# Two-layer trunk on one core: gate and up products of the MLP with the tokens stationary, turned back by 32x32 transposes and a pass through DRAM

## The chip, the core and the metric

The kernel runs on 1 core of one Trainium2 chip. The metric is the device time of one execution in microseconds (us); before the change the median of three runs is 2818.43 us (2815.97 to 2819.57).

## The reference, cut to what matters

The model is a trunk of two layers over 256 tokens of width 2048, all in float32. The part that the change concerns is the gated MLP, once per layer:

```python
D_MODEL = 2048; SEQ = 256; D_FF = 5632; CONV_WIDTH = 3

def causal_dwconv(u, w):          # depthwise over positions, width 3
    y = up[:, 0:L] * w[0]         # up: u with two zero rows in front
    for k in range(1, CONV_WIDTH):
        y = y + up[:, k:k + L] * w[k]
    return y

def conv_gated_mlp(h, w_gate, w_up, conv_w, conv_b, w_down):
    g = causal_dwconv(h @ w_gate, conv_w) + conv_b
    return (jax.nn.silu(g) * (h @ w_up)) @ w_down

def reference(...):
    for l in range(DEPTH):
...
        h = h + memory_cross_attention(rms_norm(h, norm_xattn[l]), mem_n, xa_w_q[l], xa_w_kv[l], xa_w_o[l])
        h = h + conv_gated_mlp(rms_norm(h, norm_ffn[l]), ff_w_gate[l], ff_w_up[l],
                               ff_conv_w[l], ff_conv_b[l], ff_w_down[l])
    return rms_norm(h, norm_final)
```

`rms_norm` divides each token by the root of its mean square and multiplies by a gain per channel. The mixers (a short convolution with an S5 scan in layer 0, sliding-window attention in layer 1) and the cross attention into 256 memory tokens stay as they are.

## The kernel before, in words

**Data.** Activations lie with channels on the 128 partitions and the 256 tokens along the free axis: the residual `h` is 16 tiles of 128x256. Weights are float32 in DRAM and are used once, so they stream: HBM reads come to 523 MB in the whole run.

**Precision.** Every product is computed from split operands. `wload` (lines 78-94) loads one block of weights (1 MB: 16 k of 128x128, or four k of 128x512) into a `raw` buffer by one DMA on SyncE's queue, and splits it in pieces of 1024 columns: ScalarE casts to `hi` (line 90, type float32r), VectorE takes the rest to `lo` (line 91). There are three raw buffers and four buffers each of hi and of lo pieces, enough for two blocks. Activations are split in the same way into operand tiles `op` of 128x512: hi in the first 256 columns, lo in the last (`split`, `split_gain`, lines 63-76; 32 such tiles).

**A tile of a product.** `gemm` (119-156) goes over output tiles of 128 channels. The weights are stationary and the tokens move: per k one matmul of hi against hi and lo of the tokens (line 105, 512 columns), then per k one of lo against hi of the tokens (line 110, 256 columns). The left and right halves of the PSUM bank are summed afterwards (`add_halves`, 158-161: a copy by ScalarE, an add by VectorE). There are four PSUM banks for this (`pp`) and four for all else (`pm`). Two parameters of `gemm` cover the end of the stage ahead: `pre` tiles are started with all k but the last `late`, which come after.

**The order.** The program is written as straight Python. The framework fixes the order of each engine's instructions ahead of time by its own model of durations, under the data dependences and the buffers that come free; it isn't program order. Each engine, and each DMA queue (SyncE's and ScalarE's), then works strictly in its order.

**The MLP** (`mlp`, 910-958) takes the 16 operand tiles `xs` of the normed residual. The norm's factor per token isn't in them: it is computed from sums of squares (`stat_add`, `stat_col`, `stat_bc`: 168-218) as a column per token and, by a small matmul, as a tile `rbc` that holds it along the tokens on every partition. `pairs` computes gate and up tile by turns. `evac_gate` (916-926) sums the halves, multiplies by rbc (GpSimd, line 919), convolves over tokens (lines 921-923), applies silu and multiplies by rbc again (line 925), since the up tile is taken unscaled; `evac_up` (928-932) sums its halves, multiplies by the gate's result (line 931) and splits it into an operand tile for the down product. The 44 channel tiles go in four slabs of 11; after each slab one pair of the next, then the down product over that slab's 11 k, added to `h` (`resid_part`, 960-963). The last slab's down product goes through `resid_evac` (279-295), which adds to `h`, squares for the next norm (line 174, summed by GpSimd in line 172) and, in layer 0, splits the next stage's operands (`split_gain`, lines 67 and 68).

**A product of the other form** stands in the cross attention's values (`mem_kv`, 311-329): there the memory tokens are stationary, 128 at a time, and weights 512 wide move. Per 512 channels there are two PSUM banks (tokens 0-127 and 128-255); each block of four k has 16 matmuls with hi weights (lines 319, 320) and 8 with lo (line 324). The result has tokens on partitions; ScalarE scales it by a factor per token on the way out of PSUM (line 328) and writes it to DRAM. That is done ahead of the layers, at 135 to 440 us.

## Time and profile before

| what | before |
|---|---|
| median of three runs | 2818.43 us |
| the profiled execution | 2817.71 us |
| its span, first to last instruction | 2815.9 us |
| granted TensorE clock, mean | 0.997 |
| instructions | 42249 |
| DMA packets, bytes, mean rate | 89788, 536.63 MB, 191 GB/s |
| queue of SyncE (q1), share of the 16 engines' time | 52.7% |
| queue of ScalarE (q10), the same | 0.9% |

A profile is of one execution. Engines in its rows: PE is TensorE's matmuls, PEld its loads of the stationary operand (beside the matmuls), DVE VectorE, ACT ScalarE, POOL GpSimd, SP SyncE; a q behind an engine's name is its sequencer or queue. L105 is line 105 of the kernel. A group of instructions reads: line, engine, operation, output<-inputs, shapes, count | busy us, mean ns of one | idle time of the engine just before them, and what ended it. A row of waits reads: who waited <- for whom: us in total, times, longest. A row of a time line reads: start, length, engine, line, operation, and how many are merged. Matmuls overlap in the records, so their pace is read from start to start. A row of windows reads: stretch, its length, busy us of PE, PEld, DVE, ACT and POOL with counts, granted clock, mean busy share of the 16 DMA engines, GB/s. A row of DMA issues reads: what, queue, count, KB each, median us from issue to landing.

### The profile page before, as it was taken

What the parts mean: (1) busy time and instruction counts of PE and PEld (TensorE: products, weight loads), DVE (VectorE), ACT (ScalarE), POOL (GpSimd) and SP (SyncE); (2) the same over time, 40 slices, a digit from 0 to 9 for tenths busy, and PEclk for the clock granted to TensorE, in tenths of its full rate; (3) what the DMA queues carried; (4) which work ended last, traced back from release to release, by engine and by line L of the source; (5) the groups of instructions that cost most, each with busy time, mean ns of one, the idle gap of its engine ahead of it and who ended that gap; (6) DMA issues with size and microseconds to landing.
All of it is one profiled execution on the core that took longest, in us unless ns stands there. A gap on an engine that the chain in (4) does not pass through costs nothing.

```text
span 2815.9 us, 42249 instructions
## 1 busy us (share of the span) xinstructions
PE 2785.6 (99%) x16263; PEld 2438.2 (87%) x16263; DVE 1975.3 (70%) x3227; ACT 1570.8 (56%) x2544; POOL 360.5 (13%) x397
## 2 busy tenths in 40 slices
PE   9999999999999999999999999999999999999998
PEld 8787878888988888888888888889888888888887
DVE  8978788867666666666666778776666666666666
ACT  7676766655555545545445566555555455454454
POOL 2000000000012211202112310000122022021122
PEclk9999999999999999999999999999999999999999
DMA  8664665555455545455454544454455554554544
GB/s 305 204 213 172 213 226 202 201 181 210 180 177 186 193 171 212 169 206 190 169 210 176 198 171 163 150 211 179 174 185 190 174 205 168 209 192 168 206 171 143
DMA packets 89788, 536.63 MB, mean 191 GB/s; under 512 B 10641, under 2 KB 17137, under 8 KB 38641
## 3 DMA queue, kind: packets, MB, share of 16 engines
q1 hardware_dynamic: 86656, 524.66, 52.7%
q10 hardware_dynamic: 2928, 9.26, 0.9%
q8 instruction: 127, 2.08, 0.3%
q14 instruction: 77, 0.62, 0.1%
HBM read 523.35 MB, written 10.53 MB: 190 GB/s over the span
## 4 chain that ended last, share of the span: by engine, by line
PE 94%; DVE 3%; ACT 2%; DMA 1%; issue 1%; POOL 0%; SPq 0%; DVEq 0%; ACTq 0%; POOLq 0%
PE ps L105 55%; PE ps L110 29%; PE ps L319 2%; PE ps L324 2%; PE ps L320 2%; DVE lo L91 1%; PE m L882 1%; PE m L788 1%; ACT stmp L489 1%; ACT hi L90 1%; DMA kv<-kst 0%; PE m L774 0%; DVE S L494 0%; PE m L742 0%; PE m L852 0%
## 5 line engine op out<-in xcount | busy, mean ns | idle before, releaser
L105 PE MATMUL ps<-op,hi 128*128 128x512 f32 x6997 | 1689.3, 392 | 5.4 <-ACT hi L90 2.8
L105 PEld LDWEIGHTS ps<-op,hi 128*128 128x128 f32 x6997 | 1283.2, 188 | 260.5 <-ACT hi L90 5.2
L91 DVE TENSOR_TENSOR lo<-raw,hi 128x1024 fp32r<-128x1024 f32 (+2 forms) x1033 | 1200.6, 1185 | 378.4 <-ACT hi L90 154.8
L90 ACT CAST hi<-raw 128x1024 fp32r<-128x1024 f32 (+2 forms) x1033 | 1001.8, 983 | 813.0 <-PE ps L105 720.5
L110 PEld LDWEIGHTS ps<-op,lo 128*128 128x128 f32 x7008 | 903.6, 191 | 38.5 <-DVE lo L91 2.3
L110 PE MATMUL ps<-op,lo 128*128 128x256 f32 x7008 | 920.5, 283 | 1.3 <-DVE lo L91 1.3
L172 POOL TENSOR_TENSOR acc<-acc,t 128x256 f32<-128x256 f32 x98 | 90.8, 927 | 1185.7 <-ACT t L174 1181.7
L160 ACT COPY t<-ps 128x256 f32<-128x256 f32 x290 | 106.9, 370 | 166.5 <-PE ps L110 163.6
L919 POOL TENSOR_TENSOR t<-t,rbc 128x256 f32<-128x256 f32 x88 | 68.8, 781 | 748.7 <-DVE t L161 720.9
L922 DVE SCALAR_TENSOR_TENSOR t<-t,ff_conv 128x255 f32<-128x255 f32 x88 | 42.9, 487 | 141.9 <-ACT t L921 141.9
L925 POOL TENSOR_TENSOR t<-t,rbc 128x256 f32<-128x256 f32 x88 | 109.5, 1244 | 216.2 <-ACT t L924 216.2
L68 DVE SCALAR_TENSOR_TENSOR op<-h,gains,op 128x256 fp32r<-128x256 f32 x96 | 72.8, 765 | 85.1 <-ACT op L67 85.0
L489 ACT ACTIVATE stmp<-S,s_pw 128x256 f32<-128x256 f32 (+3 forms) x256 | 116.8, 522 | 27.6 <-DVE S L496 21.6
L75 DVE TENSOR_TENSOR op<-t,op 128x256 fp32r<-128x256 f32 x104 | 43.8, 425 | 118.6 <-ACT op L74 118.2
L161 DVE TENSOR_TENSOR t<-ps,t 128x256 f32<-128x256 f32 x250 | 103.8, 415 | 0.9 <-ACT t L160 0.9
L319 PE MATMUL ps<-hi,op 128*128 128x512 f32 x256 | 101.0, 394 | 0.3 <-ACT hi L90 0.2
L320 PE MATMUL ps<-hi,op 128*128 128x512 f32 x256 | 99.8, 390 | 0.0
L931 POOL TENSOR_TENSOR t<-t 128x256 f32<-128x256 f32 x88 | 67.2, 764 | 135.0 <-DVE t L161 134.7
L74 ACT CAST op<-t 128x256 fp32r<-128x256 f32 x104 | 41.9, 406 | 50.7 <-POOL t L931 43.3
L494 DVE TENSOR_TENSOR S<-S,stmp 128x512 f32<-128x512 f32 (+11 forms) x92 | 60.6, 663 | 13.0 <-ACT stmp L489 12.8
L324 PE MATMUL ps<-lo,op 128*128 128x512 f32 x256 | 63.6, 390 | 0.7 <-DVE lo L91 0.7
L921 ACT ACTIVATE t<-t,ff_b,ff_conv 128x256 f32<-128x256 f32 x88 | 52.3, 595 | 20.7 <-POOL t L919 20.7
(213 smaller groups left out, 1494.9 us busy)
## 6 DMA issues: line engine op xcount, KB each, us to landing
raw<-in_ff_gate SPq DMA_DIRECT2D x88, 1024.0 KB, 4.8
raw<-in_ff_up SPq DMA_DIRECT2D x88, 1024.0 KB, 4.8
raw<-in_ff_down SPq DMA_DIRECT2D x128, 704.0 KB, 4.0
raw<-in_xa_k SPq DMA_DIRECT2D x32, 1024.0 KB, 4.9
raw<-in_xa_v SPq DMA_DIRECT2D x32, 1024.0 KB, 5.3
raw<-in_xa_q SPq DMA_DIRECT2D x32, 1024.0 KB, 4.8
raw<-in_xa_o SPq DMA_DIRECT2D x32, 1024.0 KB, 4.8
raw<-in_ev_w_in SPq DMA_DIRECT2D x28, 1024.0 KB, 4.9
```

Of the source, the lines that this page charges most:

```text
L90: nc.scalar.copy(hi, s)
L91: nc.vector.tensor_tensor(lo, s, hi.bitcast(F32), op=ALU.subtract)
L105: nc.tensor.matmul(ps, lhsT=hi, rhs=o, start=k == 0, stop=False)
L110: self.nc.tensor.matmul(ps[:, :T], lhsT=w[k][1], rhs=ops[k][:, :T], start=False, stop=k == K - 1)
L160: self.nc.scalar.copy(t, ps[:, T:])
L161: self.nc.vector.tensor_tensor(out, ps[:, :T], t, op=ALU.add)
L172: nc.gpsimd.tensor_tensor(self.acc, self.acc, self.sq, op=ALU.add)
L319: nc.tensor.matmul(ps[b], lhsT=o[:, b * P:(b + 1) * P], rhs=w[j][0], start=k == 0, stop=False)
L320: nc.tensor.matmul(ps[b], lhsT=o[:, T + b * P:T + (b + 1) * P], rhs=w[j][0], start=False, stop=False)
L324: nc.tensor.matmul(ps[b], lhsT=self.memop[k][:, b * P:(b + 1) * P], rhs=w[j][1], start=False, stop=k == KT - 1)
L489: nc.scalar.activation(tmp[:, x, :, p - p0, :], at(0, both, p), AF.Copy, scale=pw[:, x, k, 8 * b + p:8 * b + p + 1])
L925: nc.gpsimd.tensor_tensor(y, y, self.rbc, op=ALU.mult)
```

## The change

Of the 44 channel tiles of gate and up, the first 40 (`NTOK`) are computed in 10 chunks of 512 channels with the tokens stationary; the last four stay as they were.

- The tokens stand in `xs` in even-odd order: first the 128 even tokens, then the 128 odd ones. `split_gain` and the last `resid_evac` of the cross attention write them so (reads with a step of two, writes contiguous). So `stat_col`, `stat_bc` and `add_halves` get a `turned` form that undoes or follows it.
- `tok_gemm` is the product: per 512 channels two banks (even and odd tokens), four blocks of weights, each of 16 matmuls with hi and 8 with lo, 512 columns moving in all of them. The weights of gate and up are packed for it as blocks of four k by 512 channels, 8 KB contiguous per partition as before.
- `tok_turn` brings the result back to channels on partitions: ScalarE copies each bank out, scaled by the norm's factor per token; VectorE transposes it in blocks of 32x32, writing even and odd tokens by turns; four DMAs on ScalarE's queue write it to DRAM, 32 partitions each, in pieces of 64 floats (256 B); one DMA on SyncE's queue reads it back as four channel tiles of 128x256, in pieces of 1 KB.
- Since the factor is applied on the way out of PSUM, GpSimd's two products with rbc fall away for these tiles. Convolution, silu, product and split stay.
- The slabs of the down product become 12, 12, 12 and 8 k; each comes one chunk (the last one four pairs) after the tiles that it uses. The last has `late=1, pre=2`.

The core of the diff:

```diff
-SLAB = 11
+NTOK = 40
...
+        self.dz = pool("dramz", 4, space=DRAM)
...
-    def split_gain(self, src, gcol):
+    def split_gain(self, src, gcol, turned=False):
         nc = self.nc
         o = self.op_tile()
-        nc.scalar.activation(o[:, :T], src, AF.Copy, scale=gcol)
-        nc.vector.scalar_tensor_tensor(o[:, T:], src, gcol, o[:, :T].bitcast(F32), op0=ALU.mult, op1=ALU.subtract)
+        hi, lo = o[:, :T], o[:, T:]
+        if turned:
+            src = src.rearrange("p (m b) -> p b m", b=2)
+            hi, lo = (x.rearrange("p (b m) -> p b m", b=2) for x in (hi, lo))
+        nc.scalar.activation(hi, src, AF.Copy, scale=gcol)
+        nc.vector.scalar_tensor_tensor(lo, src, gcol, hi.bitcast(F32), op0=ALU.mult, op1=ALU.subtract)
         return o
...
+    def tok_gemm(self, src, xs, after=None):
+        nc = self.nc
+        ps = [self.pp.tile([P, 512], F32, name="ps", tag="ps") for _ in range(2)]
+        for q in range(4):
+            w = self.wload(src(q), 4, 512)
+            for j in range(4):
+                k = 4 * q + j
+                for b in range(2):
+                    for i in range(2):
+                        nc.tensor.matmul(ps[b], lhsT=xs[k][:, i * T + b * P:i * T + (b + 1) * P], rhs=w[j][0], start=k == 0 and i == 0, stop=False)
+            for j in range(4):
+                k = 4 * q + j
+                for b in range(2):
+                    nc.tensor.matmul(ps[b], lhsT=xs[k][:, b * P:(b + 1) * P], rhs=w[j][1], start=False, stop=k == KT - 1)
+            if after is not None:
+                after(q)
+        return ps
+
+    def tok_turn(self, pool, ps, rcol, tag):
+        nc = self.nc
+        tt = pool.tile([P, 16, 32, 2], F32, name="tt", tag="tt")
+        for b in range(2):
+            z = pool.tile([P, 512], F32, name="zt", tag="zt")
+            nc.scalar.activation(z, ps[b], AF.Copy, scale=rcol[:, b:b + 1])
+            nc.vector.transpose(tt[:, :, :, b], z.rearrange("p (j i) -> p j i", i=32))
+        zd = self.dz.tile([512, T], F32, name="zd", tag="zd")
+        for q in range(4):
+            nc.scalar.dma_start(zd.rearrange("(j i) (q e) -> q i j e", i=32, q=4)[q], tt[32 * q:32 * q + 32].rearrange("p j i b -> p j (i b)"))
+        zf = pool.tile([P, 4, T], F32, name="zf", tag=tag)
+        nc.sync.dma_start(zf, zd.rearrange("(n p) t -> p n t", p=P))
+        return zf
...
+        def chunk(c):
+            first = c == 0
+
+            def after(q):
+                if first and q == 0:
+                    st["rcol"] = self.stat_col(turned=True)
+                if first and q == 2:
+                    self.stat_bc(turned=True)
+            g = self.tok_turn(pool, self.tok_gemm(lambda q: I["ff_gate_t"][l, c, q], xs, after), st["rcol"], "zg")
+            ys = []
+            for i in range(4):
+                n = 4 * c + i
+                z = g[:, i, :]
+                y = pool.tile([P, T], F32, name="y", tag="y")
+                nc.scalar.activation(y, z, AF.Identity, scale=cw[:, l, n, 2:3], bias=cb[:, l, n:n + 1])
+                v.scalar_tensor_tensor(y[:, 1:], z[:, :T - 1], cw[:, l, n, 1:2], y[:, 1:], op0=ALU.mult, op1=ALU.add)
+                v.scalar_tensor_tensor(y[:, 2:], z[:, :T - 2], cw[:, l, n, 0:1], y[:, 2:], op0=ALU.mult, op1=ALU.add)
+                nc.scalar.activation(y, y, AF.Silu)
+                ys.append(y)
+            u = self.tok_turn(pool, self.tok_gemm(lambda q: I["ff_up_t"][l, c, q], xs), st["rcol"], "zu")
+            for i in range(4):
+                nc.gpsimd.tensor_tensor(u[:, i, :], u[:, i, :], ys[i], op=ALU.mult)
+                st["ops"].append(self.split(u[:, i, :]))
+
+        def down(s, k0, k1, cur):
             if s == 3:
                 evac, nxt = self.resid_evac(gnext)
             else:
-                ev, _ = (lambda n, ps: self.resid_part(n, ps)), None
-                evac = ev
-
-            self.gemm(lambda n: I["ff_down"][l, s, n], range(16), cur, SLAB, evac, one=lambda n: s == 3 and gnext is None and n == KT - 1)
...
+                evac, nxt = self.resid_part, None
+
+            self.gemm(lambda n: I["ff_down"][l, n][:, k0:k1, :], range(16), cur, k1 - k0, evac, late=1 if s == 3 else 0, pre=2 if s == 3 else 0, one=lambda n: s == 3 and gnext is None and n == KT - 1)
+            return nxt
...
+            ops = st["ops"] = []
+            for c in range(4):
+                chunk(c)
+            down(0, 0, 12, ops[:12])
+            for c in range(4, 7):
+                chunk(c)
+            down(1, 12, 24, ops[12:24])
+            for c in range(7, 10):
+                chunk(c)
+            down(2, 24, 36, ops[24:36])
+            for n in range(NTOK, NFF):
+                pair(n)
+            return down(3, 36, 44, ops[36:])
```

The buffers of the turned results (`pool`, two per tag, six for `y`) live for the length of one layer's MLP.

More of the change, by code (lines that the diff above doesn't have):

```diff
@@ L185, in stat_col @@
             c = slice(b * P, (b + 1) * P)
-            nc.tensor.matmul(ps[:, b:b + 1], lhsT=self.acc[:, c], rhs=self.ones[:, :1], start=True, stop=not apart)
+            nc.tensor.matmul(ps[:, b:b + 1], lhsT=self.tokens(self.acc, b) if turned else self.acc[:, c], rhs=self.ones[:, :1], start=True, stop=not apart)
             if apart:
@@ L205, in rsqrt_col, with stat_bc @@
         return y
-    def stat_bc(self, tag="h", copy=True):
+    def stat_bc(self, tag="h", turned=False):
         nc = self.nc
@@ L215, in stat_bc @@
         rbc = self.smp.tile([P, T], F32, name="rbc", tag="rbc_" + tag, bufs=1)
-        nc.scalar.copy(rbc, pb[:, :T])
+        if turned:
+            nc.scalar.copy(rbc.rearrange("p (m b) -> p b m", b=2), pb[:, :T].rearrange("p (b m) -> p b m", b=2))
+        else:
+            nc.scalar.copy(rbc, pb[:, :T])
         self.rbc = rbc
@@ L929, in evac_up @@
             z = self.t1()
[L930 removed]
+            self.add_halves(z, ps, turned=True)
             nc.gpsimd.tensor_tensor(z, z, st["y"], op=ALU.mult)
             st["ops"].append(self.split(z))
[L934 to L937 removed]
@@ L939, in mlp, with pair @@
-        nxt = None
-        ops = []
-        st["ops"] = ops
-        pairs(range(0, SLAB), pre=2)
-        for s in range(4):
-            cur = ops
-            if s < 3:
-                ops = []
-                st["ops"] = ops
-                pairs(range(SLAB * (s + 1), SLAB * (s + 1) + 1))
+        def pair(n):
+            w = n - NTOK
+            self.gemm(lambda i: I["ff_up" if i else "ff_gate"][l, w], (0, 1), xs, KT, lambda i, ps: (evac_up if i else evac_gate)(n, ps))
+        def chunk(c):
[20 more added lines that the diff above has]
+                st["ops"].append(self.split(u[:, i, :]))
```

41 lines of the change are left out of this document (23 added, 18 removed).

## The prediction

> **What bounds the kernel now.** I read the page first (engines, chain), then who waits for TensorE, then one tile of the stage in the order of time.
>
> ```profile
> PE 2785.6 (99%) x16263; PEld 2438.2 (87%) x16263; DVE 1975.3 (70%) x3227; ACT 1570.8 (56%) x2544; POOL 360.5 (13%) x397
> PE 94%; DVE 3%; ACT 2%; DMA 1%; issue 1%; POOL 0%; SPq 0%; DVEq 0%; ACTq 0%; POOLq 0%
> PE m L214 <- DVE t L212: 9.0, 2, 6.3
> PE ps L105 <- DVE op L75: 1.1, 2, 0.6
> ```
>
> Row 1: the matmul engine is busy for 99% of the span; the next engine, VectorE (DVE), for 70%. Row 2: 94% of the chain that ended last is matmuls. Rows 3 and 4 (waits; total us, times, longest) show how little TensorE waits: L214 is the norm's broadcast; the wait for an operand of a `down` product (L75 makes it) is 1.1 us in both layers. So a stage gets shorter only by less TensorE time, and every new wait of TensorE comes on top.
>
> One gate or up tile (128 channels, 256 tokens) now, start and length in us:
>
> ```profile
> 1003.50 3.82 PE L105 MATMUL ps<-op,hi 128*128 128x512 f32 x16
> 1007.15 2.08 PE L110 MATMUL ps<-op,lo 128*128 128x256 f32 x16
> 1009.07 2.68 PE L105 MATMUL ps<-op,hi 128*128 128x512 f32 x11
> ```
>
> Start to start it takes 1009.07 - 1003.50 = 5.57 us, without a gap. And the form that the change brings in already runs here: the cross attention's value projection (L319, L320, L324) has the tokens stationary and weights 512 wide moving. One of its blocks (four k of 512 channels: the same products as one tile) is 16 matmuls with hi and 8 with lo:
>
> ```profile
> 173.61 0.39 PE L319 MATMUL ps<-hi,op 128*128 128x512 f32 x1
> 173.84 0.39 PE L320 MATMUL ps<-hi,op 128*128 128x512 f32 x1
> ...
> 177.01 0.39 PE L320 MATMUL ps<-hi,op 128*128 128x512 f32 x1
> 177.24 1.98 PE L324 MATMUL ps<-lo,op 128*128 128x512 f32 x8
> 179.05 0.39 PE L319 MATMUL ps<-hi,op 128*128 128x512 f32 x1
> ```
>
> (Twelve rows between the second and third are alike.) A block takes 179.05 - 173.61 = 5.44 us.
>
> **The change, part by part.**
>
> *Matmuls.* Both forms move 16 x (512 + 256) = 24 x 512 = 12288 columns, but in 24 instructions for 32. Those 32 - 24 = 8 explain the difference: lo now takes (1009.07 - 1007.15) / 16 = 120.0 ns for 256 columns, L324 (179.05 - 177.24) / 8 = 226.3 ns for 512, so a matmul costs 2 x 120.0 - 226.3 = 13.7 ns whatever its width, and 8 x 13.7 = 0.11 us of the 0.13. The change turns 40 of 44 channel tiles of gate and of up in two layers: 40 x 2 x 2 = 160 tiles into 160 blocks. Gain 160 x (5.57 - 5.44) = 20.8 us; with 0.01 us of reading error in each figure 17.6 to 24. I take 20.
>
> The Trainium skill ("TensorE: Matmul & The Clock Gate", Part 1) gives a warm matmul as N / 2.4 GHz plus about 2.5 ns. By that figure, as an estimate, a tile would take 16 x (215.8 + 109.2) = 5.20 us and a block 24 x 215.8 = 5.18, and the gain would be 3 us. The two rows above speak against it; I go by them.
>
> *Leaving PSUM.* Per result of 512 channels: out go four tiles' copies and adds (L160, L161) and in the gate and up the products with rbc (L919, L925); in come two scaled copies of 128x512 (the shape of L328) and two 32x32 transposes.
>
> ```profile
> L160 ACT COPY t<-ps 128x256 f32<-128x256 f32 x290 | 106.9, 370 | 166.5 <-PE ps L110 163.6
> L161 DVE TENSOR_TENSOR t<-ps,t 128x256 f32<-128x256 f32 x250 | 103.8, 415 | 0.9 <-ACT t L160 0.9
> L925 POOL TENSOR_TENSOR t<-t,rbc 128x256 f32<-128x256 f32 x88 | 109.5, 1244 | 216.2 <-ACT t L924 216.2
> L328 ACT ACTIVATE kst<-ps,rcol x16: 670/682/690, 182.0 to 440.8; 128x512 f32<-128x512 f32 x16
> L91 DVE TENSOR_TENSOR lo<-raw,hi 128x1024 fp32r<-128x1024 f32 (+2 forms) x1033 | 1200.6, 1185 | 378.4 <-ACT hi L90 154.8
> L309 ACTq DMA_DIRECT2D kv<-kst x8: 326/326/327, 85.8 to 351.7; - x8
> L452 SPq DMA_DIRECT2D craw<-in_s5c x4: 551/556/643, 79.1 to 367.2; - x4
> ```
>
> ScalarE (ACT): 4 x 0.37 = 1.48 us becomes 2 x 0.68 = 1.36, plus four DMA issues at 0.33 (L309) to 0.64 us (L452, the longest three-dimensional one), 1.3 to 2.6 us in 21.8. VectorE: 4 x 0.415 = 1.66 us goes; a transpose of 512 elements has no row and lies between 0.415 (256 elements) and 1.19 us (L91, about 1024), 0.8 to 2.4 us for two; I take 1.4, near 512-wide work. GpSimd only loses. No engine nears TensorE. This part costs nothing, because ScalarE runs ahead and waits for TensorE to free weight buffers:
>
> ```profile
> ACT hi L90 <- PE ps L105: 720.5, 489, 3.5
> ```
>
> *The way through DRAM: the queues.* The writes (four per result, ScalarE's queue) wait for the second transpose; behind them stand casts of weights (L90), for which TensorE waits in the end. The read back (SyncE, SP) waits for all four writes; behind it on SP stand the weight loads. How early they are issued decides:
>
> ```profile
> 854.26 0.33 SPq L82 DMA_DIRECT2D raw<-in_ff_gate  x1
> 874.57 3.59 PE L105 MATMUL ps<-op,hi 128*128 128x512 f32 x15
> L90 ACT CAST hi<-raw 128x1024 fp32r<-128x1024 f32 (+2 forms) x1033 | 1001.8, 983 | 813.0 <-PE ps L105 720.5
> raw<-in_ff_gate SPq DMA_DIRECT2D x88, 1024.0 KB, 4.8
> kv<-kst ACTq DMA_DIRECT2D x16, 512.0 KB, 6.8
> ```
>
> The first gate tile's weights are issued 874.57 - 854.26 = 20.3 us before their first matmul; less 4.8 to land and 0.98 (L90) and 1.19 (L91) for its first casts, SP may stand still for some 13 us. A write of as many bytes takes 6.8 us here, in pieces of 4 KB. If SP stands only for that, nothing reaches TensorE. The results themselves have time: a `down` never uses the newest chunk, so there lie two results (44 us) between, and ahead of the last `down` four pairs.
>
> *The way through DRAM: the 16 DMA engines.* Per result 512 KB are written in 2048 pieces of 256 B and read in pieces of 1 KB.
>
> ```profile
> 76.00:85.00 9.00, 9.00 (x55) 8.04 (x54) 8.62 (x50) 3.92 (x6) 0.00 (x0) 1.00 0.72 214
> 1005.00:1009.00 4.00, 4.00 (x27) 3.61 (x26) 1.60 (x3) 2.37 (x4) 1.33 (x2) 1.00 0.50 184
> 1671.00:1677.00 6.00, 6.00 (x38) 5.29 (x37) 4.26 (x14) 3.74 (x10) 0.41 (x1) 1.00 0.68 224
> 2100.00:2400.00 300.00, 300.00 (x1725) 264.96 (x1724) 193.43 (x264) 152.56 (x224) 56.45 (x62) 1.00 0.53 185
> bias<-fd SPq DMA_DIRECT2D x16, 256.0 KB, 3.6
> ff_b<-in_ff_b SPq DMA_DIRECT2D x1, 44.0 KB, 4.6
> sinks<-in_sinks SPq DMA_DIRECT2D x1, 16.0 KB, 3.7
> ```
>
> In the first four rows the last two columns are the DMA share and GB/s. The MLP (row 4) needs 0.53; at the faster pace 0.54, of a result's 4 x 5.44 = 21.8 us about 11.8, and 10.0 stay free. Weights alone (row 2) cost 4 x 0.50 / (4 x 0.184 MB) = 2.72 us per MB. Row 3 holds one load of weights (1.05 MB) and one of the bias in 1 KB pieces (0.26 MB): 6 x 0.68 - 2.85 = 1.23 us, so the 512 KB read costs at most 2.5 us. For the write the low end is the weights' rate, 0.52 x 2.72 = 1.4 us. For the high end row 1: between 76 and 85 us, 9 x 0.72 = 6.5 us of DMA time carried 1.93 MB, among it four loads of constants of 128 pieces each, 8 to 352 B long (ff_b, q_b, k_b, sinks; 0.07 MB). Taking the rest at the weights' rate leaves 6.5 - 1.86 x 2.72 = 1.4 us, for 512 / 16 = 32 pieces per engine about 45 ns each; 128 of them per engine and result are 5.8 us. Together 3.9 to 8.3 us of the free 10.0: it fits. I take no cost in time.
>
> *The down products.* Slabs of 12, 12, 12 and 8 in place of 4 x 11: the same matmuls. The last slab of layer 0 has only 8 k, and the work per tile beside it stays (rows 2 to 4 are those of 1535 to 1595 us, the last slab before; row 1 is of the page):
>
> ```profile
> L172 POOL TENSOR_TENSOR acc<-acc,t 128x256 f32<-128x256 f32 x98 | 90.8, 927 | 1185.7 <-ACT t L174 1181.7
> L91 DVE TENSOR_TENSOR lo<-raw,hi 128x1024 fp32r<-128x1024 f32 x15 | 19.8, 1326 | 10.6 <-ACT t L174 5.9 <-PE ps L110 3.4 <-ACT hi L90 1.2
> L68 DVE SCALAR_TENSOR_TENSOR op<-h,gains,op 128x256 fp32r<-128x256 f32 x10 | 8.2, 817 | 0.0
> L288 DVE TENSOR_TENSOR h<-h,ps 128x256 f32<-128x256 f32 x11 | 4.5, 409 | 0.0
> ```
>
> TensorE needs 8 / 16 x 5.57 = 2.78 us per tile, VectorE 1.33 + 0.82 + 2 x 0.41 = 2.97: there VectorE becomes the bound, (2.97 - 2.78) x 16 = 3 us. Ends: 0, where the finished buffers ahead cover it; 14, if also L91's idle time, 10.6 / 15 = 0.7 us, stays with each tile. I take 3. (Layer 1 has no L68.) The new `late=1, pre=2` there covers the 1.1 us of row 4 of the first fence: -0.5 in each layer.
>
> *Entry of the MLP, strided reads.* The statistics now come after one block (5.4 us) and before after two tiles of 15 k (10 us); the chain behind the last residual tile (two L288, square, two sums) is 2 x 0.41 (L288), a square like L160's 0.37 and 2 x 0.93 (L172), about 3 us: hidden, 0 to 2 us. Split, add and rbc with a step of two have no row; they run beside 5.57 us of TensorE per tile with over 1 us to spare, at 0, even at double length.
>
> *Turn-by-turn waits.* 40 results, each a place where copy, transposes, four issues and one read come between casts and loads. The nearest row is the value projection, where TensorE waited for hi and lo in L319 and L324:
>
> ```profile
> PE ps L324 <- DVE lo L91: 0.7, 1, 0.7
> PE ps L319 <- ACT hi L90: 0.2, 1, 0.2
> ```
>
> That is 0.9 us for 8 results, 0.11 each, with the S5 scan beside it: 40 x 0.11 = 4.5 us at the high end, 0 at the low; I take 2.
>
> Sum: -20 + 3 - 1 + 2 = -16 us (ends: -25 and +3). The profiled execution took 2817.7 us (span 2815.9 and 1.8 around it), so 2801.7; the median of the three runs, 2818.4, lies 0.7 above it: 2802.4, say 2802.
>
> **Rivals.**
>
> *The DMA engines become the bound (slower).* A 256 B write could cost more than any row here allows, since no row has one. It decides from (10.0 - 2.5) / 128 = 59 ns a piece; at 70 ns a result needs 11.8 + 2.5 + 9.0 = 23.3 us, 1.5 more than TensorE, x 40 = +60, about 2862; at 94 ns, twice the bound, 11.8 + 2.5 + 12.0 = 26.3, +4.5 x 40 = 180, about 2982. For it: 45 ns isn't far from 59, and those pieces were loads. Against: a part of those 45 ns belongs to the starts of nine DMAs, and 256 B are near the long end of those pieces. The Trainium skill ("DMA: Bandwidth & Descriptors", Specifications) has transfers below 512 B done as read-modify-write. If that doubled a piece, the low end would become 2.9 us (the sum stays) and the high end 11.6, this rival. Chance 0.10.
>
> *SP's wait takes its place.* The order on SP is fixed beforehand. If the read back stands at its earliest, right behind the last block, SP waits for two copies and a transpose (3 us with queueing), four issues (2.6) and the writes (6.8, plus 5.8 - 1.4 = 4.4 if they cost the high end): 17 us, 4 more than the 13 of slack; 40 x 4 = +160, about 2962, and any excess over 0.4 us per result gives back the whole 16 us. For it: all loads share that queue. Against: it needs both the early place and slow writes. Chance 0.11, mostly with an excess of one or two us (2840 to 2880).
>
> *No change.* Waits of 0.3 to 0.55 us per result eat the gain, or the 13.7 ns aren't per matmul (then the 3 us worked out above, against 4 of costs): 2813 to 2824. Chance 0.12.
>
> **How the numbers follow.** The forecast has the rest, 0.67, and its own range is 2796 to 2812. What a measurement can tell from no change is 0.2%, 5.6 us. Faster 0.67, same 0.12, slower 0.11 + 0.10 = 0.21. For 8 in 10 the range takes in the forecast, the no-change case and the small excesses of SP's wait: 2796 to 2832.
>
> **What would show it.** Right: blocks of 5.44 us with 24 matmuls, about 14980 matmuls in all (16263 - 160 x 8), TensorE still at 99%, DMA share 0.65 to 0.9 in the chunks, loads landing later than 4.8 us without anyone waiting on TensorE's side. Wrong: TensorE waiting for hi or lo once per result with SP's queue behind the read (second rival); DMA share at 1.0 through the chunks and loads landing ever later (first); blocks at 5.55 us (third); gaps in the last slab of layer 0 of over 3 us (the VectorE term).

## The result and the profile after

The changed kernel takes 2796.26 us (median of four runs, 2794.98 to 2797.57); the kernel before, 2817.88 us over its four runs. The ratio is 0.9924, with a 95% interval of 0.9906 to 0.9941: 21.6 us faster, where 16 were forecast. The profiled execution took 2794.98 us, its span 2793.2 us, 22.7 less than the span before.

First the page of the kernel after: engines, chain, and the queue that now carries the writes. Then the waits on TensorE's side (total us, times, longest).

```profile
PE 2766.6 (99%) x14980; PEld 2373.2 (85%) x14980; DVE 1928.5 (69%) x3115; ACT 1556.8 (56%) x2432; POOL 212.8 (8%) x237
PE 94%; DVE 3%; ACT 2%; issue 1%; DMA 0%; SPq 0%; DVEq 0%; ACTq 0%
q10 hardware_dynamic: 87408, 30.24, 4.2%
```
```profile
PE m L263 <- DVE t L261: 8.7, 2, 6.0
PE ps L110 <- ACT hi L95: 2.8, 4, 1.3
```

TensorE is still the bound at 99%, with 1283 matmuls fewer and 19 us less busy time. The largest waits stand nearly as before (8.7 us at the norm's broadcast, where it was 9.0, and 2.8 us for hi in products of the old form, as before). No wait names the lines of the new product (L179, L183) or its results' operands (L80): whatever the pass through DRAM costs, TensorE doesn't see it. ScalarE's queue has gone from 2928 packets and 0.9% of the 16 DMA engines' time to 87408 and 4.2%.

One block of the new product, on TensorE's time line of the kernel after (start, length):

```profile
999.55 3.79 PE L179 MATMUL ps<-hi,op 128*128 128x512 f32 x16
1003.17 1.98 PE L183 MATMUL ps<-lo,op 128*128 128x512 f32 x8
1004.99 1.29 PE L179 MATMUL ps<-hi,op 128*128 128x512 f32 x5
```

From start to start 1004.99 - 999.55 = 5.44 us, where a tile took 5.57. Read off the time lines in the same way, from the first matmul of an MLP to the first one behind it, the two MLPs account for nearly all of the gain. These are the two ends of layer 1's MLP before, then after:

```profile
2064.16 3.59 PE L105 MATMUL ps<-op,hi 128*128 128x512 f32 x15
2801.22 0.28 PE L186 MATMUL m<-ones,acc 128*128 128x1 f32 x2
```
```profile
2051.89 3.82 PE L179 MATMUL ps<-hi,op 128*128 128x512 f32 x16
2778.00 0.28 PE L235 MATMUL m<-ones,acc 128*128 128x1 f32 x2
```

| stretch | before | after | difference |
|---|---|---|---|
| MLP of layer 0 | 874.57 to 1611.48 = 736.91 | 873.45 to 1599.46 = 726.01 | -10.90 |
| MLP of layer 1 | 2064.16 to 2801.22 = 737.06 | 2051.89 to 2778.00 = 726.11 | -10.95 |
| ahead of, between and behind them | | | -0.85 |

### The profile page after: what moved, and what is told of

The parts are those of the page before. It is cut to its first block, busy times and chain, and to the rows that moved or that the text cites. A ratio compares the mean times of both kernels' runs of the same rounds, so it can differ in the third digit from the quotient of the medians.

```text
span 2793.2 us, 39738 instructions
## 1 busy us (share of the span) xinstructions
PE 2766.6 (99%) x14980; PEld 2373.2 (85%) x14980; DVE 1928.5 (69%) x3115; ACT 1556.8 (56%) x2432; POOL 212.8 (8%) x237
## 3 DMA queue, kind: packets, MB, share of 16 engines
q10 hardware_dynamic: 87408, 30.24, 4.2%
## 4 chain that ended last, share of the span: by engine, by line
PE 94%; DVE 3%; ACT 2%; issue 1%; DMA 0%; SPq 0%; DVEq 0%; ACTq 0%
PE ps L110 35%; PE ps L179 21%; PE ps L115 18%; PE ps L183 10%; PE ps L371 2%; PE ps L372 2%; PE ps L376 2%; DVE lo L96 1%; PE m L934 1%; ACT stmp L541 1%; PE m L840 1%; ACT hi L95 1%; PE m L826 0%; PE m L794 0%; DVE S L546 0%
## 5 line engine op out<-in xcount | busy, mean ns | idle before, releaser
L96 DVE TENSOR_TENSOR lo<-raw,hi 128x1024 fp32r<-128x1024 f32 (+1 forms) x1001 | 1155.6, 1176 | 579.0 <-issue 221.4
L95 ACT CAST hi<-raw 128x1024 fp32r<-128x1024 f32 (+1 forms) x1001 | 994.4, 1008 | 897.9 <-PE ps L110 443.0
L110 PE MATMUL ps<-op,hi 128*128 128x512 f32 x4440 | 1078.2, 393 | 3.4 <-ACT hi L95 2.8
L110 PEld LDWEIGHTS ps<-op,hi 128*128 128x128 f32 x4440 | 813.6, 189 | 167.1 <-ACT hi L95 5.1
L179 PE MATMUL ps<-hi,op 128*128 128x512 f32 x2560 | 607.0, 389 | 0.0
L115 PEld LDWEIGHTS ps<-op,lo 128*128 128x128 f32 x4448 | 575.4, 191 | 25.4 <-DVE lo L96 1.4
L115 PE MATMUL ps<-op,lo 128*128 128x256 f32 x4448 | 588.4, 283 | 0.6 <-DVE lo L96 0.6
L179 PEld LDWEIGHTS ps<-hi,op 128*128 128x128 f32 x2560 | 480.0, 188 | 99.3
L183 PE MATMUL ps<-lo,op 128*128 128x512 f32 x1280 | 316.1, 389 | 0.0
L183 PEld LDWEIGHTS ps<-lo,op 128*128 128x128 f32 x1280 | 240.3, 188 | 49.9
L1012 POOL TENSOR_TENSOR zf<-zf,y 128x256 f32<-128x256 f32 x80 | 75.1, 969 | 1095.6 <-DMA zf<-zd 1056.1
L371 PE MATMUL ps<-hi,op 128*128 128x512 f32 x256 | 101.0, 394 | 0.3 <-ACT hi L95 0.2
L372 PE MATMUL ps<-hi,op 128*128 128x512 f32 x256 | 99.8, 390 | 0.0
L206 ACT COPY t<-ps 128x256 f32<-128x256 f32 x130 | 47.4, 367 | 53.4 <-PE ps L115 50.4
L80 DVE TENSOR_TENSOR op<-zf,op 128x256 fp32r<-128x256 f32 x80 | 49.3, 628 | 32.5 <-ACT op L79 32.5
L376 PE MATMUL ps<-lo,op 128*128 128x512 f32 x256 | 63.6, 390 | 0.7 <-DVE lo L96 0.7
L371 PEld LDWEIGHTS ps<-hi,op 128*128 128x128 f32 x256 | 48.0, 188 | 12.8 <-ACT hi L95 1.6
```

Source lines behind the costliest of these rows:

```text
L95: nc.scalar.copy(hi, s)
L96: nc.vector.tensor_tensor(lo, s, hi.bitcast(F32), op=ALU.subtract)
L110: nc.tensor.matmul(ps, lhsT=hi, rhs=o, start=k == 0, stop=False)
L115: self.nc.tensor.matmul(ps[:, :T], lhsT=w[k][1], rhs=ops[k][:, :T], start=False, stop=k == K - 1)
L179: nc.tensor.matmul(ps[b], lhsT=xs[k][:, i * T + b * P:i * T + (b + 1) * P], rhs=w[j][0], start=k == 0 and i == 0, stop=False)
L183: nc.tensor.matmul(ps[b], lhsT=xs[k][:, b * P:(b + 1) * P], rhs=w[j][1], start=False, stop=k == KT - 1)
```

## The experiments

The theory: a matmul has a fixed cost beside its width, the change saves 8 of 32 matmuls per block, and the way through DRAM lies wholly beside TensorE. Its rivals: that the gain comes from something else in the change (the slabs, the loads' form), and that the hidden pass is near a limit, which might be the DMA engines, SyncE's stand behind the writes, or, as it turned out, ScalarE. Each ratio is to the kernel before, run on the same chip.

| run | what it changes | median us | ratio (95% interval) |
|---|---|---|---|
| lo_halves | after, lo in 16 matmuls of 256 | 2817.01 | 0.9994 (0.9985 to 1.0003) |
| all_halves | after, 48 matmuls of 256 per block | 2846.67 | 1.0102 (1.0086 to 1.0117) |
| slabs_only | before, with the new slabs alone | 2816.56 | 0.9993 (0.9984 to 1.0002) |
| no_dram | after, without the pass through DRAM | 2797.17 | 0.9923 (0.9910 to 0.9935) |
| all44 | after, all 44 tiles in the new form | 2793.86 | 0.9911 (0.9897 to 0.9924) |
| natural | after, tokens in their own order, 128 B pieces | 2810.00 | 0.9970 (0.9958 to 0.9983) |
| pieces64 | after, 64 B pieces | 2878.10 | 1.0209 (1.0195 to 1.0223) |
| raw2_before | before, two raw buffers | 2834.34 | 1.0058 (1.0045 to 1.0072) |
| raw2_after | after, two raw buffers | 2834.58 | 1.0061 (1.0044 to 1.0077) |
| natural_pool | natural, writes issued by GpSimd | 2796.91 | 0.9926 (0.9913 to 0.9938) |
| pieces64_pool | pieces64, writes issued by GpSimd | 2797.36 | 0.9927 (0.9914 to 0.9941) |
| pieces64_read | pieces64, read back issued by GpSimd | 3050.36 | 1.0823 (1.0796 to 1.0850) |

### Is it the number of matmuls?

**lo_halves** gives back the 8 matmuls and keeps all else:

```diff
-                    nc.tensor.matmul(ps[b], lhsT=..., rhs=w[j][1], ...)
+                    for c in range(2):
+                        s = slice(c * 256, (c + 1) * 256)
+                        nc.tensor.matmul(ps[b][:, s], lhsT=..., rhs=w[j][1][:, s], ...)
```

> The kernel after, but the 8 lo matmuls of each block go as 16 of 256 columns, so that a block has 32 instructions again, as a tile had before; products, order and all else stay. Theory A (the gain is a fixed 13.7 ns per matmul, 8 fewer in each of 160 blocks): 160 x 8 x 13.7 ns = 17.5 us come back, 2814 us (2811 to 2817), blocks of 5.55 us. Rival B (the gain comes from the rest: fewer waits, less work on GpSimd, other slabs): 2796 us, within 2.

One block of it on TensorE's time line:

```profile
1002.36 3.82 PE L179 MATMUL ps<-hi,op 128*128 128x512 f32 x16
1006.01 2.08 PE L185 MATMUL ps<-lo,op 128*128 128x256 f32 x16
1007.92 1.32 PE L179 MATMUL ps<-hi,op 128*128 128x512 f32 x5
```

The block takes 1007.92 - 1002.36 = 5.56 us, and the whole gain is gone: 2817.01 - 2796.26 = 20.8 us for 1280 more matmuls, 16 ns each, where theory A's 13.7 ns gave 17.5 us. The products, the pass through DRAM and the turned results are all still there.

**all_halves** goes on in the same direction: the hi matmuls, too, are halved (but for the first of each bank), 3760 more matmuls than after.

> The kernel after with both the hi and the lo matmuls of the blocks as halves of 256 columns (but for the first of each bank), so that a block has 48 instructions for 24. Halving lo alone cost 20.8 us. Theory A (a fixed cost per matmul): 24 more per block at 13.7 ns are 53 us, in proportion to the measured 20.8 us 62: 2849 to 2859 us, blocks of 5.75 to 5.85 us. Rival B (the lo halves cost for another reason, as a change between 512 and 256 columns at each end of a run): 2796 to 2830 us.

```profile
1002.41 4.00 PE L185 MATMUL ps<-hi,op 128*128 128x256 f32 x32
1006.25 2.08 PE L191 MATMUL ps<-lo,op 128*128 128x256 f32 x16
1008.17 1.01 PE L185 MATMUL ps<-hi,op 128*128 128x256 f32 x7
```

5.76 us per block, and 2846.67 - 2796.26 = 50.4 us for 3760 matmuls: 13.4 ns each. The time follows the count, down and up, but not at one price: the step from lo_halves is 2846.67 - 2817.01 = 29.7 us for 2480 matmuls, 12.0 ns each, and so the run came out 2.3 us below theory A's range. Each of these matmuls has its own load of the stationary operand beside it; whether the fixed cost is the matmul's or that load's, these runs don't split.

**slabs_only** asks whether the slabs carry part of it: the kernel before with slabs of 12, 12, 12 and 8 and the last one's `late=1, pre=2`, nothing turned.

```diff
-SLAB = 11
+SLABS = (0, 12, 24, 36, 44)
...
+            k0, k1 = SLABS[s], SLABS[s + 1]
+            self.gemm(lambda n: I["ff_down"][l, n][:, k0:k1, :], range(16), cur, k1 - k0, evac, late=1 if s == 3 else 0, pre=2 if s == 3 else 0, ...)
```

> The kernel before with only the slabs changed: 12, 12, 12 and 8 k for 4 x 11, and two tiles started ahead of the last operand in the last slab. Theory A (nearly all of the gain is in the blocks): 2817 us, at most 1 us faster than before for the operand's wait; the 3 us that were forecast for VectorE in the last slab don't show. Rival B (the slabs bring part of the 21.6 us): 2805 to 2813 us.

Its ratio can't be told from 1. Its time line lets one say more: its MLPs take 875.04 to 1611.14 = 736.10 us and 2064.92 to 2801.11 = 736.19, 0.8 and 0.9 us less than before. lo_halves, with the same slabs and the same 32 matmuls per block but the new form, takes 2798.56 - 2062.36 = 736.20 in layer 1:

```profile
2062.36 3.82 PE L179 MATMUL ps<-hi,op 128*128 128x512 f32 x16
2798.56 0.28 PE L237 MATMUL m<-ones,acc 128*128 128x1 f32 x2
```

So with as many matmuls the new form gains nothing and costs nothing; the slabs with their late k and first tiles bring some 0.9 us per MLP, and the 8 matmuls the rest: (736.20 - 726.11) / 80 blocks / 8 = 15.8 ns each.

### Does the pass through DRAM cost anything?

**no_dram** takes the transposed tile as it lies:

```diff
-        tt = pool.tile([P, 16, 32, 2], F32, name="tt", tag="tt")
+        tt = pool.tile([P, 16, 32, 2], F32, name="tt", tag=tag)
...
-        zd = self.dz.tile([512, T], F32, name="zd", tag="zd")
-        for q in range(4):
-            nc.scalar.dma_start(zd..., tt...)
-        zf = pool.tile([P, 4, T], F32, name="zf", tag=tag)
-        nc.sync.dma_start(zf, zd.rearrange("(n p) t -> p n t", p=P))
-        return zf
+        return tt.rearrange("p j i b -> p (j i b)").rearrange("p (n t) -> p n t", t=T)
```

> The kernel after without the pass through DRAM: the 32x32 transposed tile is used as it lies in place of what is read back, so the four writes and the read of each result are left out and gate and up hold other channels and tokens than in the reference. Copies, transposes and all later work stay. Theory A (the pass is hidden, queues and DMA engines have room): 2796 us, within 1.5. Rival B (each of 40 passes costs TensorE some tenths of a us through SyncE's queue or ScalarE's): 2780 to 2792 us.

2797.17 us against 2796.26 with the pass; the MLP of layer 1 takes 726.11 us in both. The pass is wholly hidden from TensorE. What it uses of the DMA engines shows in the windows over the first chunks, of after and then of no_dram (stretch, length, busy us of five engines, granted clock, DMA share, GB/s):

```profile
900.00:1065.00 165.00, 165.00 (x751) 137.53 (x751) 102.12 (x126) 89.71 (x121) 13.07 (x13) 1.00 0.71 235
```
```profile
900.00:1065.00 165.00, 165.00 (x747) 137.33 (x747) 102.98 (x131) 91.34 (x127) 12.79 (x16) 1.00 0.55 186
```

The share rises by 0.16: 165 x 0.16 = 26.4 us for the eight results that are written and read back between 899.1 and 1064.2 us, 3.3 us of all 16 engines per result. In the mean of this stretch the DMA engines aren't near full.

**all44** turns the last four tiles as well (`NTOK = 44`, 11 chunks, no untouched pair left).

> The kernel after with all 44 channel tiles of gate and up in 11 chunks; the third slab's down product lies between the last chunk and the last slab. Theory A: 16 tiles more become blocks at 0.13 us each, 2.1 us, so 2794 us (2793 to 2796), if the last chunk's way through DRAM is hidden by the 67 us of the third slab's product. Rival B (the last result comes late, or operand buffers run short: 20 operand tiles live beside the normed residual): TensorE waits ahead of the last slab, 2798 to 2815 us.

2793.86 us, the lowest median of all; its interval (0.9897 to 0.9924) overlaps that of after, so the further 2 us aren't shown. In layer 1 its MLP takes 724.63 us, 1.5 less than after; in layer 0 as much is saved (724.54 against 726.01), and it comes back as one wait of TensorE in the next stage:

```profile
PE ps L110 <- DVE op L73: 2.0, 1, 2.0
```

### How near is the limit, and which one?

**natural** leaves the tokens in their own order. Then a piece that is contiguous in DRAM is 32 floats (128 B), there are 4096 pieces per result, and eight DMAs write them:

```diff
-            nc.vector.transpose(tt[:, :, :, b], z.rearrange("p (j i) -> p j i", i=32))
+            nc.vector.transpose(tt[:, b], z.rearrange("p (j i) -> p j i", i=32))
...
-            nc.scalar.dma_start(zd.rearrange("(j i) (q e) -> q i j e", i=32, q=4)[q], ...)
+            for b in range(2):
+                nc.scalar.dma_start(zd.rearrange("(j i) (b q e) -> b q i j e", i=32, q=4, b=2)[b, q], tt[32 * q:32 * q + 32, b])
```

> The kernel after without the even-odd order: the two banks hold tokens 0 to 127 and 128 to 255, reads of the residual have no step, and each result is written to DRAM in 4096 pieces of 128 B by eight DMAs in place of 2048 of 256 B by four. In the profile after, ScalarE's queue has 3.3% more of the engines' time for 81920 pieces more, 18 ns each. Theory A (DMA engines have room): 256 pieces per engine at 18 ns are 4.6 us, 11.8 + 2.5 + 4.6 = 18.9 of 21.8 us per result, no change: 2796 us, within 2. Rival B (the order was needed: eight issues hold up ScalarE, or the pieces cost over 29 ns and the DMA engines become the bound): 2805 to 2860 us.

**pieces64** keeps the even-odd order and the four DMAs, but writes 8192 pieces of 16 floats (64 B) per result:

```diff
-            nc.scalar.dma_start(zd.rearrange("(j i) (q e) -> q i j e", i=32, q=4)[q], tt[...].rearrange("p j i b -> p j (i b)"))
+            nc.scalar.dma_start(zd.rearrange("c t -> (c t)").rearrange("(i x q e) -> q i x e", x=64, q=4, e=16)[q], tt[...].rearrange("p j i b -> p (j i b)").rearrange("p (x e) -> p x e", e=16))
```

> The kernel after with each result written in 8192 pieces of 64 B in place of 2048 of 256 B, as many bytes in as many DMAs; channels and tokens come back in another order than the reference's, all else stays. This looks for the point where the DMA engines become the bound, forecast at 7.5 us of writing per result. If a piece costs 18 ns whatever its length, 512 per engine take 9.2 us, 11.8 + 2.5 + 9.2 = 23.5 against 21.8 us: 40 x 1.7 = 68 us more, 2864 us, DMA share near 1.0 in the chunks. If pieces cost by their bytes: 2796 us.

natural gives up 13.7 us against after (2810.00 - 2796.26), which is in rival B's range and not in theory A's. pieces64 gives up 81.8, but not for the reason that was expected. Its row of the same window:

```profile
900.00:1065.00 165.00, 158.38 (x680) 128.81 (x679) 91.74 (x114) 81.60 (x116) 9.56 (x12) 0.98 0.73 213
```

The DMA engines are at 0.73, not at 1.0, and TensorE is idle for 6.6 us of the 165. The granted clock is lower too, 0.98 for 1.00 in after: over both MLPs TensorE is idle for 53 us, and in ten stretches of 3.4 or 6.8 us, 37 us together, the clock is at 0.50, which costs about half of that, 19 us. after has 0.1 us of such idle time and no such stretch. So the 81.8 us are in the main these waits and a clock that was lower in the same stretch of the run. Where the waits come from, the time line over all engines shows:

```profile
996.67 7.46 ACTq L199 DMA_DIRECT2D zd<-tt  x3
...
1004.23 3.88 ACT L95 CAST hi<-raw 128x1024 fp32r<-128x1024 f32 x4 [9.26 <-DMA zd<-tt]
...
1005.33 3.01 PE L179 MATMUL ps<-hi,op 128*128 128x512 f32 x8 [2.27 <-ACT hi L95]
```

ScalarE (ACTq) is in its own issues of the writes until 1004.1; only then comes the next cast of weights, which stood behind them, after 9.26 us without one; and the matmul that needs it starts after a wait of 2.27 us. Here is how long an issue takes (shortest, median, longest in ns) in after, natural and pieces64, one fence each:

```profile
L199 ACTq DMA_DIRECT2D zd<-tt x160: 309/540/1525, 899.1 to 2625.8; - x160
```
```profile
L200 ACTq DMA_DIRECT2D zd<-tt x320: 309/520/4404, 897.8 to 2638.6; - x160
```
```profile
L199 ACTq DMA_DIRECT2D zd<-tt x160: 559/1370/5485, 900.7 to 2710.5; - x160
```

The long issue is one of each series, in the same place each time: in pieces64 the second of four (3.0 to 5.5 us, median 4.4), in natural the fifth of eight (2.0 to 4.4, median 3.4). Both are the first with 2048 pieces of the series ahead of them; in after a whole series has 2048, and no issue takes over 1.53. A series takes 2.3 us by the median in after (2.2 to 3.8), 7.6 in natural (5.9 to 8.9) and 7.7 in pieces64 (6.3 to 8.7). The series are as long in natural as in pieces64, and cost a sixth: ScalarE's longest idle time before a cast that a DMA of the writes ended is 8.6 us there and 9.8 here. That the casts' lead ends in between would fit, and isn't shown.

**raw2_after and raw2_before** take the lead away instead: two raw buffers in place of three (`self.rawp = pool("raw", 2)`), in the changed kernel and in the kernel before.

> The kernel after with two raw weight buffers in place of three. SyncE's queue stands 7.2 us per result for the writes (290 us in 40 reads, the longest 10.1), and the third buffer gives loads 5.4 us more lead. Theory A (the stand is hidden by the lead of the loads, 13 us before): with about 8 us of lead the longer stands reach TensorE, 1 to 3 us for a part of the 40 results: 2805 to 2880 us, with waits for hi behind loads of weights. Rival B (the lead isn't used up, the stand would not matter): 2796 us plus what the kernel before loses with two buffers.

> The kernel before with two raw weight buffers in place of three, as a measure for the same edit on the kernel after. Theory A (lead of 13 us, of which 8 stay and nothing on SyncE's queue waits for writes in the MLP): 2818 us, within 5. Rival B (loads are late with two buffers in any form of the products): as much slower as the kernel after becomes.

That the kernel before would stay as it is was wrong: it loses 16 us of its own. Those lie ahead of the MLP, whose first matmul moves from 874.57 to 890.50; its MLPs take 737.63 us in layer 0 (890.50 to 1628.13), 0.7 more than with three, and 737.04 in layer 1. The changed kernel's take 734.08 (893.72 to 1627.80) and 740.63, 8.1 and 14.5 more than with three buffers. Against the old form with two buffers it is 3.6 us faster in layer 0 and as much slower in layer 1: with two buffers the gain is gone in the sum and in the median. (These are single executions, and raw2_after's times spread from 2829.66 to 2842.07 us.) ScalarE's waits for landing weights in raw2_after:

```profile
ACT hi L95 <- DMA raw<-in_ff_down: 157.7, 73, 6.5
ACT hi L95 <- DMA raw<-in_ff_gate_t: 76.7, 31, 4.5
```

So the third raw buffer is part of what hides the pass. Whether SyncE's stand behind the writes or the later landing of loads uses it up, this pair doesn't split.

**natural_pool and pieces64_pool** let GpSimd, which is busy for 8% of the span, issue the writes (`nc.gpsimd.dma_start` for `nc.scalar.dma_start`); the access patterns with their pieces stay.

> The kernel with natural token order and 4096 pieces of 128 B per result, with the eight writes issued from GpSimd's queue in place of ScalarE's. With ScalarE issuing it took 2810 us: its queue was busy with the eight issues for 7 to 8 us per result (2.2 to 3.3 us in the kernel after), and behind them the casts of weights were late. Theory A (the cost is ScalarE standing in its issues): 2796 to 2799 us, no wait for hi in the chunks. Rival B (the pieces themselves are too many for the DMA engines, or SyncE waits too long for them): 2806 to 2815 us, as from ScalarE.

> The kernel with 8192 pieces of 64 B per result, with the four writes issued from GpSimd's queue in place of ScalarE's; channels and tokens come back in another order than the reference's. From ScalarE it took 2878 us, with 7 to 8 us of issues per result and a DMA share of only 0.73 in the chunks, so the engines weren't the bound that had been expected. Theory A (ScalarE standing in its issues): most of the 82 us goes, 2796 to 2815 us. Rival B (the engines or SyncE's wait for the writes, 10.5 us per result and up to 12.8): 2860 to 2890 us.

Both lose nothing against after: 2796.91 and 2797.36 us. In pieces64_pool the same result in pieces of 64 B is now free, at a DMA share of 0.77 (first fence, the window), and GpSimd takes about 1.08 us for each issue, with no long ones (second fence, ns; a series of four takes 4.2 us). The third fence is GpSimd's queue (packets, MB, share of the 16 engines):

```profile
900.00:1065.00 165.00, 165.00 (x747) 137.36 (x746) 100.99 (x127) 89.41 (x122) 43.77 (x44) 1.00 0.77 234
```
```profile
L199 POOL DMA_DIRECT2D zd<-tt x160: 1025/1076/1186, 901.2 to 2630.3; - x160
```
```profile
q0 software_dynamic: 7680, 20.98, 4.8%
```

That the engines carry 0.77 here without anyone waiting speaks against them as the limit of pieces64 at 0.73. But the pair changes more than who issues. The bytes travel in 7680 packets, where ScalarE's queue in pieces64 has 333168, 330240 of them more than in the kernel before, and they cost 4.8% of the engines' time for 7.0. And SyncE's order changed with it: its stand behind the writes fell from 419.8 us to 31.0. So this pair alone doesn't separate ScalarE's stand from SyncE's, nor the issuing engine from the packets.

**pieces64_read** was to separate the two stands: the writes go back to ScalarE, and the read back moves from SyncE to GpSimd, so that SyncE never stands behind the writes.

> The kernel with 8192 pieces of 64 B per result, written from ScalarE's queue as at first (2878 us), with only the read back moved from SyncE's queue to GpSimd's; channels and tokens come back in another order than the reference's. Moving the writes to GpSimd (2797 us) also took SyncE's wait for them from 420 to 31 us, so it doesn't say which of the two queues mattered. Theory A (ScalarE stands in its issues and the casts behind them are late): nothing is gained, 2865 to 2885 us. Rival B (SyncE stands for the writes and the weight loads behind are late): most of the 82 us goes, 2796 to 2815 us.

Neither expectation gave its time: 3050.36 us, 172 more than pieces64. SyncE has no wait for the writes any more, and nothing is faster. Alone that doesn't clear SyncE, since moving the read brought waits of its own; but ScalarE's waits for landing weights of the MLP speak against it (after first, then pieces64):

```profile
ACT hi L95 <- DMA raw<-in_ff_down: 24.3, 12, 4.0
```
```profile
ACT hi L95 <- DMA raw<-in_ff_down: 27.9, 13, 5.8
```

For the weights of gate and up neither has such a wait, and in pieces64 the next cast begins within 0.33 us of the end of each of the 40 series of issues, 0.1 by the median. So SyncE's stand of 419.8 us made hardly any weights late, and that theory falls.

What stays as it was in pieces64_read is ScalarE's idle time before casts that a DMA of the writes ended, 299.3 us here (first row; in pieces64 296.4, also 34 times). What is new are the read's own waits, of GpSimd, of ScalarE for the results, and of TensorE for hi:

```profile
ACT hi L95 <- DMA zd<-tt: 299.3, 34, 10.1
POOL zf L201 <- DMA zd<-tt: 1157.3, 39, 85.2
ACT y L1005 <- DMA zf<-zd: 124.5, 20, 7.9
ACT op L79 <- POOL zf L1012: 177.1, 80, 9.6
PE ps L179 <- ACT hi L95: 112.6, 28, 5.1
```

GpSimd stands in order behind the writes, its products (L1012) behind that, and ScalarE, in order too, stands behind those results with casts behind it. The granted clock is lower again (0.93 between 900 and 1065 us, where after has 1.00). Read as for pieces64, the two MLPs hold 172 us of TensorE's idle time, 118 more, and 167 us at a clock of 0.50, 129 more, which cost about 65; together that is a little more than the 176 us between the two profiled executions.

## Why the prediction was right, and which terms were off

The mechanism was the one forecast. That the time itself fell into the range was close: 2796.26 us lies 0.26 above the lower end of both ranges, the forecast's own and the one for 8 in 10, because every term beside the matmuls came out lower than forecast. That the number came out inside is in part luck; the direction doesn't hang on it.

**The bound and the pace: right.** TensorE was and is the bound, a block takes 5.44 us as the value projection's rows said, and the count fell by 1283 against the 1280 forecast. The 20 us for it are confirmed in size (10.1 us per MLP) and in cause: put the matmuls back and the gain goes. The price per matmul was read a little low from the two rows, 13.7 ns for 15.8 in the MLP of layer 1. The Trainium skill ("TensorE: Matmul & The Clock Gate", Part 1) gives about 2.5 ns per warm matmul beside its width; this case's runs don't agree, with 12 to 16 ns in split float32 products that each load their own stationary operand. The measurement decides: by the page's 2.5 ns the change would have been worth 3 us, as an estimate, and it brought 21.6.

**VectorE in the last slab, +3: mis-sized, it is 0 in this run and up to 2.0 us in its relatives.** The step was sized right as a pace: VectorE was the bound there. Its groups in that slab of the kernel after (1555 to 1599 us, layer 0):

```profile
L96 DVE TENSOR_TENSOR lo<-raw,hi 128x1024 fp32r<-128x1024 f32 x17 | 21.7, 1279 | 0.6 <-ACT hi L95 0.5 <-PE ps L115 0.2
L73 DVE SCALAR_TENSOR_TENSOR op<-h,gains,op 128x256 fp32r<-128x256 f32 x14 | 12.4, 890 | 0.0
L340 DVE TENSOR_TENSOR h<-h,ps 128x256 f32<-128x256 f32 x15 | 6.1, 409 | 1.2 <-PE ps L115 1.2
L341 DVE TENSOR_TENSOR h<-h,ps 128x256 f32<-128x256 f32 x14 | 5.6, 409 | 0.0
```

Per tile 1.28 + 0.89 + 2 x 0.41 = 2.99 us and nearly no idle time, against 2.79 of TensorE (1593.88 to 1596.67). So TensorE should have had to wait within the slab, and it doesn't: what can come late is an operand of the next stage, and that stage's first tile begins with the operands that are there and gives VectorE time for the rest. The low end of the term, 0 by the finished buffers ahead, is what came. What remains shows in six of the twelve runs with the new slabs as one wait in that tile, 0.4 to 2.0 us (1.0 in slabs_only, 2.0 in all44); in after there is none. `late` and `pre` were forecast at -1; with the slabs they gave -1.7 in slabs_only. So slabs and edges together were +2 in the sum and about -1.7 on the chip.

**Turn-by-turn waits, +2: 0.** no_dram has the same MLP, to the hundredth of a microsecond, and TensorE waits for no operand of the new products. The value projection's 0.11 us per result was no price of the form. These terms, with the -0.85 us outside the MLPs that no step forecast (no more than executions of one kernel differ by), make the difference between -16 and -22.7.

**SyncE's wait: right that it is hidden.** The kernel after, SyncE's wait for the writes and how long the loads take to land (us, median):

```profile
SPq L201 <- DMA zd<-tt: 290.0, 64, 10.1
```
```profile
raw<-in_ff_gate_t SPq DMA_DIRECT2D x80, 1024.0 KB, 5.7
raw<-in_ff_up_t SPq DMA_DIRECT2D x80, 1024.0 KB, 5.9
```

290.0 us over 40 results are 7.25 each, in no single wait over 10.1: below the 13 us of slack, although loads land 1 us later than before, as forecast. The 13 us were read at one place, the entry of the MLP. The slack hangs on the third raw buffer; without it the gain went in the sum, by this wait or by the later landings.

**The DMA engines: right that it fits, wrong about the limit.** Write and read took 3.3 us per result, below the low end of the bounds (3.9). A 256 B piece costs (4.2 - 0.9)% x 16 x 2793 us / 81920 = 18 ns of an engine, against a threshold of 59; by bytes at the weights' rate it would be 11. The Trainium skill ("DMA: Bandwidth & Descriptors", Specifications) has transfers below 512 B done as read-modify-write; the trace agrees that such pieces are dearer by the byte, 1.6 times, and no run here shows by what mechanism. Smaller pieces cost less each: 128 B (5.5 - 0.9)% x 16 x 2803 / 163840 = 12.6 ns, 64 B (7.9 - 0.9)% x 16 x 2875 / 327680 = 9.8 ns. With four times the pieces the engines still had a quarter of their time free. As the rival was worded, its mechanism doesn't decide anywhere in these runs.

**The limit that the prediction passed over is ScalarE.** It priced the four issues at 1.3 to 2.6 us, they took 2.3 by the median (2.2 to 3.8), and it called them free since ScalarE runs ahead; that is so here. But this is the nearest edge that these runs found: in natural and pieces64 a series of about 8 us holds back the casts behind it, and TensorE waits for hi. In natural that is 10.6 us in ten waits before L110, where after has 2.8 in four; the six that are new stand in the first three down products of each layer, one in each. Its profiled execution is the fastest of its six, 10.2 us slower than after's; by the medians it is 13.7. The even-odd order, which halves the pieces and the DMAs, is worth 13.7 us as long as ScalarE issues them, and nothing (0.9926 against 0.9924) when GpSimd does, with its other packets. The Trainium skill ("DMA: Bandwidth & Descriptors", Issuing engines are not separate DMA queues) says that another issuing engine saves only sequencer time, usually small beside the DMA. That it is sequencer time fits; that it is small doesn't for 64 B pieces: a series of issues holds ScalarE for 7.7 us of the 11.2 from the first issue to the last landing (medians). Moving it to GpSimd was worth 2878.10 - 2797.36 = 80.7 us, packets included.

## What to carry to other kernels

Where matmuls fill the span, count them: the same products with fewer, wider matmuls were faster by 12 to 16 ns for each one saved, and the neighbouring stage that already used the wide form gave the pace beforehand. A detour that TensorE never waits for costs nothing, but price it on every in-order queue that it passes, the issue of its DMAs on a busy engine included, since a series of issues in small pieces can stand for 8 us with weights behind it. A lag at the end of a stage costs only what the next stage gives no time to catch up.

## What the runs showed that was not expected

- Of a series of writes in small pieces from ScalarE one issue is long, the first with 2048 pieces ahead of it: 3.0 to 5.5 us in pieces64, 2.0 to 4.4 in natural, where the shortest issues take 0.56 and 0.31. From GpSimd each takes nearly the same, 0.65 us for 512 pieces of 128 B and 1.08 for 2048 of 64 B, and the bytes go in far fewer packets. What ScalarE's issue waits for isn't visible; that a queue fills up would fit, and wasn't tested.
- In the two runs in which TensorE waits most, its granted clock is lower as well: it was 0.50 in ten stretches of 3.4 or 6.8 us in the MLPs of pieces64 and in 35 in those of pieces64_read, and in none in after.
- A 32x32 transpose of 128x512 with a step of two on its output takes as long as ScalarE's copy of the same size (shortest, median, longest in ns, in the kernel after):

```profile
L196 DVE STREAM_TRANSPOSE tt<-zt x80: 666/688/711, 897.8 to 2623.6; 128x512 f32<-128x512 f32 x80
```
- A raw buffer less costs the kernel before 16 us ahead of the MLP and 0.7 us in it.
